# Two written forms for each expert turn of the second layer

## The chip, the core and the metric

The kernel runs on one core of one Trainium2 chip. The metric is the device time of one execution in microseconds. TensorE (PE) multiplies, ScalarE (ACT) and VectorE (DVE) work on rows, GpSimd (POOL) has nothing to do in the stage that is changed, and SyncE (SP) issues the loads of weights. Each engine runs its own list of instructions in order, by its own sequencer, and waits for the others at semaphores. A branch on a value known only at run time is taken by every engine for itself.

## The reference, cut to what matters

A block of two layers; each mixes tokens and then sends every token to two of sixteen experts. The change concerns the experts of the second layer, where only the 256 latent tokens are left.

```python
def moe_ffn(h, w_router, router_bias, w_gate, w_up, w_down):
    ...   # best group of four experts, then the two best experts in it; gates sum to one
    y = jnp.zeros_like(h)
    for e in range(N_EXPERTS):                      # 16
        a = jax.nn.silu(h @ w_gate[e]) * (h @ w_up[e])   # 1024 -> 512
        y = y + gates[..., e:e + 1] * (a @ w_down[e])    # 512 -> 1024
    return y
```

Everything is float32. An expert's weights are 6 MB.

## The kernel before

The second layer's experts are `turns()` (L1808), sixteen turns in the fixed order `TURNS`, one expert a turn. An expert works only on the rows routed to it, in blocks of 64 (`BLK`). How many rows it has is known at run time: `next_count` (L1790) loads the count `cv` into a register on every engine and gives a hint for the coming branch (L1793).

The pieces of a turn: `mm_in` (L1466) multiplies a block of 64 rows with gate and up weights (16 calls, which the trace shows as 32 matmul records); `act` (L1479) makes silu, product and gate on ScalarE and VectorE; `spin` (L1484) transposes the result; `mm_out` (L1491) multiplies with the down weights (16 records in the profile); `where` (L1502) makes the mask of rows, by one matmul into the bank "md", of which there is one, and one VectorE instruction; `parts` (L1509) splits the product in two on VectorE and ScalarE; `add` (L1520) scatters it into the 256 rows by four matmuls and four VectorE additions. `four_fetch` (L1054) gathers a quarter of the first blocks of the next four experts, and `fetch` (L1437) gathers a second block.

A plain turn is pipelined by hand: `mm_in` of expert p with the adds of expert p-2 between (`owed`), `act`, the one-hot of the next expert, `four_fetch`, `where`, `next_count(p + 1)`, `spin`, then `mm_out` of expert p-1 (`previous()`, L1821). The weights come through rings of 1 MB tiles: `main.done(4, 2)` frees the four gate and up tiles after `mm_in`, `main.done(2)` the two down tiles of the expert before, and each frees loads that SyncE issues.

A second block of an expert is `rest` (L1796), behind the branch `cv > BLK` (L1798) at the head of the turn: fetch, `mm_in`, `act`, `where`, `spin`, `mm_out`, `parts`, `add` one after the other, with blocks over 128 behind another branch (L1805, `overflow`). The expert's first block follows, with the same weights. The last turn runs its first block ahead of the branch.

The first layer's turns (`turn_0`, L1607) have two written forms already: one branch (L1672) whose first form treats two or more blocks and whose second form, `branch.Else()`, one. There the hint (`ahead()`, L1665) stands at the end of a turn, next to the branch. `main.repeat()` issues in the second form the loads that `main.done` issued in the first; with `main.again` a ring's tile is used again under its name, so that both forms mean the same tile.

## Time and profile before

| | us |
|---|---|
| median of three runs (1374.8 to 1388.9) | 1385.39 |
| the profiled execution | 1378.21 |
| its span, first to last instruction | 1376.4 |
| TensorE busy in the span | 1186.1 (86%) |
| VectorE busy | 545.2 (40%) |
| mean granted TensorE clock | 0.931 |

The second layer's experts run from 1089 us to 1368 us of the span. In the rows, a line such as L1474 is the helper that issued an instruction, not the caller; PEq or PEldq is TensorE's sequencer. An f32 matmul is listed as PE, its weight load as PEld. The time in brackets on a timeline is the idle time of the engine ahead of the group, and what ended it.

### The profile page before, as it was taken

How to read it: one execution, taken by the hardware profiler on the slowest of the kernel's cores; microseconds unless marked ns; L12 is line 12 of the kernel's file. 1: busy time of each engine (PE TensorE's matmuls, PEld its weight loads, DVE VectorE, ACT ScalarE, POOL GpSimd, SP SyncE). 2: the span in 40 equal slices, each digit the busy share in tenths (PEclk: the TensorE clock that was granted, in tenths of full speed). 3: DMA queues.
4: the chain of work that ended last, by engine and by line, in shares of the span. 5: the costliest groups of instructions: out<-in, count | busy, mean ns of one | idle time of the engine just before them, and what ended most of it. 6: DMA issues, size and time to landing. Idle time of an engine off the chain costs nothing. (4 is left out here: it accounts for less than half of the span.)

```text
span 1376.4 us, 16893 instructions
## 1 busy us (share of the span) xinstructions
PE 1186.1 (86%) x6325; PEld 668.3 (49%) x6325; DVE 545.2 (40%) x1115; ACT 311.2 (23%) x564; POOL 314.0 (23%) x254
## 2 busy tenths in 40 slices
PE   6799999999899878988898995879987698989995
PEld 2466556677678633323333333656775433333331
DVE  5431843834522450110010038585443434434445
ACT  2422213312111311111111125314332111111112
POOL 4332102233022612111111045432335100000000
PEclk9999899999689979999999997989988799989998
DMA  9574333342375489399999835210155298958971
GB/s 356 197 268 180 103 142 108 122 154 92 138 261 214 157 313 341 86 382 386 390 389 393 338 109 220 90 64 16 64 223 229 85 366 335 418 215 338 399 309 47
DMA packets 48579, 310.91 MB, mean 226 GB/s; under 512 B 6017, under 2 KB 6209, under 8 KB 14096
## 3 DMA queue, kind: packets, MB, share of 16 engines
q1 hardware_dynamic: 41936, 292.76, 54.9%
q0 software_dynamic: 6320, 15.27, 4.3%
q8 instruction: 108, 1.77, 0.5%
q10 hardware_dynamic: 144, 0.52, 0.1%
q14 instruction: 71, 0.58, 0.1%
HBM read 297.99 MB, written 12.32 MB: 225 GB/s over the span
## 5 line engine op out<-in xcount | busy, mean ns | idle before, releaser
L576 POOL TENSOR_TENSOR ws<-w,ws 128x1024 fp32r<-128x1024 f32 x50 | 120.5, 2425 | 244.0 <-ACT ws L575 240.5
L1474 PE MATMUL b_pj<-w,HE 128*64 128x512 f32 x416 | 106.2, 646 | 24.1 <-issue 13.8
L235 PE MATMUL b_pj<-hh,ws 128*128 128x512 f32 (+1 forms) x448 | 124.0, 367 | 2.0 <-POOL ws L576 2.0
L1498 PE MATMUL b_sc<-w,rows 128*64 128x512 f32 x448 | 105.2, 610 | 2.7 <-ACT rows L1488 2.7
L666 DVE SCALAR_TENSOR_TENSOR cacc<-gl,pr,cacc 128x512 f32<-128x512 f32 (+1 forms) x120 | 91.2, 760 | 2.4
L235 PEld LDWEIGHTS b_pj<-hh,ws 128*128 128x128 f32 x448 | 79.7, 199 | 20.6 <-issue 8.7
L235 PE MATMUL b_pj<-hl,ws 128*128 128x512 f32 (+1 forms) x224 | 78.9, 352 | 0.0
L1474 PEld LDWEIGHTS b_pj<-w,HE 128*64 128x64 f32 x416 | 34.1, 147 | 84.5 <-issue 82.1
L575 ACT ACTIVATE ws<-w 128x1024 fp32r<-128x1024 f32 x50 | 52.5, 1051 | 77.4 <-PE b_pj L235 50.2
L278 POOL TENSOR_TENSOR rf<-rf,half 128x1 f32<-128x1 f32 x2 | 1.1, 561 | 297.4 <-DVE rf L277 297.4
L1536 DVE TENSOR_TENSOR x<-b_ob,x 128x512 f32<-128x512 f32 x68 | 44.0, 686 | 54.8 <-PE b_ob L1527 54.6
L1381 POOL DMA_INDIRECT sums<-y,rws x19 | 29.8, 1567 | 138.3 <-DVE y L1380 113.5
L1498 PEld LDWEIGHTS b_sc<-w,rows 128*64 128x64 f32 x448 | 31.3, 140 | 60.8 <-issue 56.3
L1474 PE MATMUL b_pj<-w,hf 128*64 128x512 f32 x224 | 56.0, 633 | 5.5 <-PEq L1798 4.9
L1474 PE MATMUL b_pj<-w,x 128*64 128x512 f32 x224 | 55.6, 618 | 5.7 <-PEq L1798 2.8
L235 PE MATMUL b_md<-w,sT 128*32 128x256 f32 x736 | 57.0, 434 | 1.3 <-DVE mT L314 1.3
L1481 DVE SCALAR_TENSOR_TENSOR X<-X,gc,b_pj 64x512 f32<-64x512 f32 x16 | 12.1, 754 | 108.9 <-ACT X L1480 108.9
L1380 DVE COPY y<-b_sc 128x512 f32<-128x512 f32 x15 | 10.4, 691 | 98.4 <-PE b_sc L1498 57.0
L235 PEld LDWEIGHTS b_pj<-hl,ws 128*128 128x128 f32 x224 | 44.5, 199 | 5.8
L1527 PE MATMUL b_ob<-st,ohT 128*128 128x512 f32 x76 | 32.3, 494 | 14.8 <-DVE st L1517 9.3
L1480 ACT ACTIVATE X<-b_pj 64x512 f32<-64x512 f32 x16 | 9.4, 589 | 157.0 <-PE b_pj L1474 150.8
L1480 ACT ACTIVATE cst<-b_pj 64x512 f32<-64x512 f32 x17 | 10.1, 592 | 141.4 <-PE b_pj L1474 141.4
(471 smaller groups left out, 2154.4 us busy)
## 6 DMA issues: line engine op xcount, KB each, us to landing
w<-in_exps_dram SPq DMA_DIRECT2D x168, 1024.0 KB
w<-in_ada_dram SPq DMA_DIRECT2D x48, 1024.0 KB
w<-in_win_dram SPq DMA_DIRECT2D x16, 1024.0 KB
hold<-in_exps_dram SPq DMA_DIRECT2D x12, 1024.0 KB
w<-in_wout_dram SPq DMA_DIRECT2D x8, 1024.0 KB
hf<-in_exps_dram SPq DMA_DIRECT2D x6, 1024.0 KB
cst<-in_exps_dram SPq DMA_DIRECT2D x6, 1024.0 KB
pr<-in_par_dram SPq DMA_DIRECT2D x2, 1461.5 KB
```

The costliest lines, as they stand in the source:

```text
L235: nc.tensor.matmul(out_, lhsT=lhsT, rhs=rhs, **kw)
L575: nc.scalar.activation(wh[:, :n], src, AF.Copy)
L576: nc.gpsimd.tensor_tensor(wl[:, :n], src, wh[:, :n].bitcast(F32), op=OP.subtract)
L666: nc.vector.scalar_tensor_tensor(ac, gl[:, :, j:j + L], R("cvw", i * 31 + j, i * 31 + j + 1), ac, op0=OP.mult, op1=OP.add)
L1380: V.tensor_copy(y, b)
L1381: nc.gpsimd.indirect_dma_start(out=sums[:, :], out_offset=bass.IndirectOffsetOnAxis(ap=row, axis=0), in_=y, in_offset=None, bounds_check=1 ...
L1474: nc.tensor.matmul(b[64 * j:64 * j + 64], lhsT=x, rhs=w[k // 2][:, at:at + 512], start=(k == 0), stop=(k == 7), tile_position=(0, 64 * j))
L1480: nc.scalar.activation(a[64:], b[:64], AF.Silu)
L1481: V.scalar_tensor_tensor(a[64:], a[64:], gate[64:], b[64:], op0=OP.mult, op1=OP.mult)
L1498: nc.tensor.matmul(b[64 * j:64 * j + 64], lhsT=aT[:, f, :], rhs=w[4 + f // 2][:, at:at + 512], start=(f == 0), stop=(f == 3), tile_positio ...
L1527: nc.tensor.matmul(b, lhsT=ohT[:, t * P:(t + 1) * P], rhs=st[h], start=(i == 0), stop=(i == len(blocks) - 1))
L1536: V.tensor_tensor(y[:, cs], b, y[:, cs], op=OP.add)
```

## The change

Each turn becomes one branch with two written forms. When the count is over 64, both blocks run interleaved: `first()` (matmul, adds, act of the first block), `fetch`, the second block's `mm_in` with the same gate and up weights, then mask, transposes, the second matmuls of the expert before and of the second block, adds, and blocks over 128 behind an inner branch. Otherwise (`branch.Else()`) the old plain turn. The last turn has the branch at its head as well. `next_count(p + 1)`, which loads the count and gives the hint, moves from ahead of `spin` to behind the two forms, so it is the last thing in a turn, next to the branch of the next. `main.done(2)` moves behind the forms too. In the form for two blocks the loads that follow the freed gate and up tiles are issued at its end, in the other one by `main.repeat()` where they were. The one-hot tiles of the second block are used again (`into=oh1`) instead of allocated, and the whole of `turns()` is issued in the order in which it is written.

```diff
--- before.py
+++ after.py
@@ -1793,71 +1793,100 @@
                 tc.mark_branch_hint_location(f"rest{p}", cv > BLK, engines=engs)
                 return cv
 
-            def rest(p, e, cv, w, oh1, last):
-
-                with tc.If(cv > BLK, label=f"rest{p}"):
-                    at, st, o = AT[(p + last) % 2], ST[p % 2], OT[(p + last) % 3]
-                    with tc.manual_schedule(engines=PE_):
-                        a1 = act(mm_in(w, fetch(oh1)), gc[:, 1, e:e + 1], AM[(p + 1) % 2])
-                        where(e, o, C("slot", 1, 2), "md")
-                        b = mm_out(w, spin(a1, at))
-                    add((parts(b, st), o))
-                    with tc.If(cv > P):
-                        overflow(e, w, cv, P, AM[(p + 1) % 2], at, st, o, into=oh1)
+            def rest(e, cv, w, oh1, temp):
+
+                with tc.If(cv > P):
+                    overflow(e, w, cv, P, *temp, into=oh1)
 
             def turns():
 
 
+
+                main.again = True
                 w = aT = owed = before = None
                 oh1 = onehot(TURNS[0], C("iota2"), off1, name="on")
-                with tc.manual_schedule(engines=ALL):
-                    cv = next_count(0)
+                cv = next_count(0)
                 for p, e in enumerate(TURNS):
                     last = p == NE - 1
                     now, nxt = four[p // 4 % 2], four[(p // 4 + 1) % 2]
                     pw, pT, w = w, aT, [main.take("exp", l, 6 * e + q) for q in range(6)]
                     x = [q[:, :, p % 4] for q in now[0]]
-
-                    def previous(between=None):
-                        b = mm_out(pw, pT, bank("sc"), between)
-                        main.done(2)
+                    o, a0, aT = OT[p % 3], AM[p % 2], AT[p % 2]
+
+                    a1, st1, o1 = AM[(p + 1) % 2], ST[(p + 1) % 2], OT[(p + 1) % 3]
+
+                    def previous():
+                        b = mm_out(pw, pT, bank("sc"))
                         return parts(b, ST[p % 2]), before
 
-                    if last:
-                        with tc.manual_schedule(engines=ALL):
-                            b0 = mm_in(w, x, between=lambda k: k in (4, 6) and add(owed, only=[k // 2 - 2]))
-                            a0 = act(b0, gc[:, 0, e:e + 1], AM[p % 2])
-                            was = where(e, OT[p % 3], C("slot", 0, 1), "md")
-                            owed = previous()
-                            aT = spin(a0, AT[p % 2])
-                            b = mm_out(w, aT, bank("sc"), lambda f: f > 1 and add(owed, only=[f - 2]))
-
-                            owed = parts(b, ST[(p + 1) % 2]), was
-                        rest(p, e, cv, w, oh1, True)
-                        with tc.manual_schedule(engines=ALL):
-                            add(owed)
-                            main.done(6)
-                        break
-                    rest(p, e, cv, w, oh1, False)
-                    with tc.manual_schedule(engines=ALL):
-                        if p % 4 == 0 and p < NE - 4:
-                            four_onehots(nxt[1], pd, p // 4 + 1)
+                    def first():
                         b0 = mm_in(w, x, between=lambda k: owed and k in (4, 6) and add(owed, only=[k // 2 - 2]))
-                        main.done(4, 2 if p else 0)
-                        a0 = act(b0, gc[:, 0, e:e + 1], AM[p % 2])
-                        oh1 = onehot(TURNS[p + 1], C("iota2"), off1, name="on")
+                        act(b0, gc[:, 0, e:e + 1], a0)
+
+                    def second(h):
+
+                        b1 = mm_in(w, h, tag="md")
+                        act(b1, gc[:, 1, e:e + 1], a1)
+
+                    def end():
+
+                        b = mm_out(w, aT, bank("sc"), lambda f: f > 1 and add(now_owed, only=[f - 2]))
+                        add((parts(b, ST[(p + 1) % 2]), o))
+
+                    if p % 4 == 0 and p < NE - 4:
+                        four_onehots(nxt[1], pd, p // 4 + 1)
+                    with tc.If(cv > BLK, label=f"rest{p}") as branch:
+                        first()
+                        h = fetch(oh1)
+                        second(h)
+                        where(e, o, C("slot", 0, 1), "md")
+                        spin(a0, aT)
                         if p < NE - 4:
                             four_fetch(nxt[0], hx, nxt[1], [p % 4])
-                        was = where(e, OT[p % 3], C("slot", 0, 1), "md")
-                        cv = next_count(p + 1)
-                        aT = spin(a0, AT[p % 2])
+                        t1 = spin(a1, h[:, :4])
                         if p:
                             now_owed = previous()
+                        b = mm_out(w, t1, bank("sc"))
+                        if last:
+                            add(now_owed)
+                        where(e, o1, C("slot", 1, 2), "md")
+                        add((parts(b, st1), o1))
+                        rest(e, cv, w, oh1, (a1, AT[(p + 1) % 2], st1, o1))
+                        if last:
+                            b = mm_out(w, aT, bank("sc"))
+                            add((parts(b, st1), o))
+                            main.done(8)
+                        else:
+                            main.done(4, 2 if p else 0)
+                            onehot(TURNS[p + 1], C("iota2"), off1, into=oh1)
+                    with branch.Else():
+                        first()
+                        if last:
+                            where(e, o, C("slot", 0, 1), "md")
+                            now_owed = previous()
+                            spin(a0, aT)
+                            end()
+                            main.repeat()
+                        else:
+                            main.repeat()
+                            onehot(TURNS[p + 1], C("iota2"), off1, into=oh1)
+                            if p < NE - 4:
+                                four_fetch(nxt[0], hx, nxt[1], [p % 4])
+                            where(e, o, C("slot", 0, 1), "md")
+                            spin(a0, aT)
+                            if p:
+                                now_owed = previous()
+                    if last:
+                        break
+                    if p:
+                        main.done(2)
+                    cv = next_count(p + 1)
                     owed = now_owed if p else None
-                    before = was
+                    before = o
 
             if l:
-                turns()
+                with tc.manual_schedule(engines=ALL):
+                    turns()
             if dump is not None:
                 for t in range(T):
                     dump(f"x{l}_{t}", xres[t])
```

## Rows read from the trace of the kernel before

**Rows 1.** Busy time by stretch: PE, PEld, DVE, ACT, POOL busy (instructions), granted clock, DMA share, GB/s

```profile
1089.28:1210.63 121.35, 112.37 (x496) 43.36 (x497) 46.70 (x80) 17.75 (x32) 0.00 (x0) 0.96 0.90 361
1210.63:1252.82 42.19, 36.15 (x157) 15.01 (x155) 13.71 (x23) 5.62 (x11) 0.00 (x0) 0.88 0.56 217
1252.82:1341.97 89.15, 83.43 (x373) 29.94 (x375) 40.31 (x68) 13.99 (x25) 0.00 (x0) 1.00 0.88 354
```

**Rows 2.** Timeline of TensorE, 1263 to 1282: start us, duration, instruction [hole before]

```profile
1263.41 3.65 PE L1498 MATMUL b_sc<-w,rows 128*64 128x512 f32 x16
1267.37 3.65 PE L1474 MATMUL b_pj<-w,hf 128*64 128x512 f32 x16 [0.31 <-PEq L1798]
...
1281.92 3.65 PE L1474 MATMUL b_pj<-w,hf 128*64 128x512 f32 x16 [0.31 <-PEq L1798]
```

**Rows 3.** TensorE's sequencer by line, 1258 to 1268: ns min/median/max, first and last start

```profile
L1792 PEldq TENSOR_LOAD <-cnt x1: 307/307/307, 1260.3 to 1260.3; - x1
...
L2065 PEldq BRANCH_PREFETCH_HINT  x1: 35/35/35, 1260.8 to 1260.8; - x1
...
L1798 PEldq COMPARE_BRANCH  x1: 2387/2387/2387, 1263.4 to 1263.4; - x1
```

**Rows 4.** The turns' branches: whole stage, then 1206 to 1208, then the first

```profile
L1798 PEldq COMPARE_BRANCH  x16: 82/3452/6124, 1085.3 to 1360.1; - x16
...
L1798 PEldq COMPARE_BRANCH  x1: 82/82/82, 1207.1 to 1207.1; - x1
...
L1798 PEldq COMPARE_BRANCH  x1: 3741/3741/3741, 1085.3 to 1085.3; - x1
```

**Rows 5.** First layer's branches: 600 to 790, and one border (735 to 744)

```profile
L1672 PEldq COMPARE_BRANCH  x11: 89/6076/6708, 600.8 to 772.3; - x11
...
L2065 PEldq BRANCH_PREFETCH_HINT  x1: 35/35/35, 737.3 to 737.3; - x1
...
L1672 PEldq COMPARE_BRANCH  x1: 6196/6196/6196, 737.8 to 737.8; - x1
```

**Rows 6.** Timeline of TensorE in the first layer, two restarts of eight

```profile
672.41 7.93 PE L1474 MATMUL b_pj<-w,HE 128*64 128x512 f32 x28 [2.33 <-DMA w<-in_exps_dram]
...
729.19 6.23 PE L1474 MATMUL b_pj<-w,HE 128*64 128x512 f32 x28 [2.81 <-issue]
```

**Rows 7.** Waits, 1085 to 1377 (us in total, times, longest); then timeline of TensorE

```profile
PE b_pj L1474 <- PEq L1798: 12.2, 9, 4.2
...
PE b_pj L1474 <- ACT st L1516: 3.2, 2, 1.6
...
PE b_pj L1474 <- DMA w<-in_exps_dram: 1.0, 2, 0.7
...
1099.54 0.46 PE L1487 MATMUL b_tp<-cst 64*128 64x64 f32 x4
...
1149.85 5.35 PE L1474 MATMUL b_pj<-w,x 128*64 128x512 f32 x16 [2.81 <-PEq L1798]
```

**Rows 8.** Timeline of TensorE, 1215 to 1241: the one second block, then its expert's first

```profile
1215.29 3.65 PE L1474 MATMUL b_pj<-w,hO 128*64 128x512 f32 x16
...
1222.30 0.38 PE L1505 MATMUL b_md<-pdT,pick 16*128 16x256 f32 x1
1224.05 0.46 PE L1487 MATMUL b_tp<-cst 64*128 64x64 f32 x4 [1.37 <-DVE cst L1481]
1224.98 5.35 PE L1498 MATMUL b_ob<-w,rows 128*64 128x512 f32 x16 [0.47 <-ACT rows L1488]
1232.60 0.47 PE L1527 MATMUL b_ob<-st,ohT 128*128 128x512 f32 x1 [2.27 <-DVE st L1517]
...
1236.21 5.41 PE L1474 MATMUL b_pj<-w,hf 128*64 128x512 f32 x16 [0.54 <-PEq L1805]
```

**Rows 9.** Timeline of TensorE in the last two turns

```profile
1336.23 1.93 PE L1474 MATMUL b_pj<-w,x 128*64 128x512 f32 x6
...
1364.77 0.71 PE L1527 MATMUL b_ob<-st,ohT 128*128 128x512 f32 x2 [3.10 <-DVEq L1798]
```

## The prediction

> **What bounds the kernel now.** I read three views of the last stage in this order. First the busy time by stretch [rows 1]: the stage starts at 1089.28 us, and TensorE is busy 112.4 of its first 121.4 us and 83.4 of 89.2 us after the one long turn, VectorE 39% and 45%. The reader is to see that TensorE's own list of instructions sets the pace and that only its holes can be won. Second TensorE's timeline across one turn border [rows 2]: the last work of a turn is the second matmul of the expert before (16 records, 3.65 us), and the next turn's first matmul stands 0.31 us behind its end; a plain turn is 14.24 us of work, 14.55 us in all (1267.37 to 1281.92). Third what TensorE's sequencer does there [rows 3]: it loads the count at 1260.3, gives the branch hint at 1260.8 and comes to the branch at 1263.4, when the 3.65 us of matmuls are queued but have only begun. The branch lasts 2.39 us and so ends 1.3 us before those matmuls do. It costs nothing because of that cover.

> The sum below is made against the profiled execution, 1378.2 us; the median of the three runs is 7.2 us above it, and I put the same change on that median.

> **What the branch costs.** All sixteen branches of the stage [rows 4]: from 0.08 to 6.12 us, median 3.45. The 0.08 us one is the only one not taken (1207.1), so exactly one expert of sixteen has more than 64 rows, the ninth turn's; fifteen turns jump. For a jump, hint to end is 2.6 + 3.45 = 6.1 us in the middle and 5.0 us in the shortest steady case [rows 3]. The hint therefore takes about 2.6 us off the branch.

> The change moves count load and hint behind the second matmul's instructions, directly ahead of the branch. The first layer is written that way already: a turn with two forms, the hint 0.5 us ahead of the branch [rows 5]. There the jumps last 6.1 us in the middle, up to 6.7, and the branch also starts as the last matmuls begin. TensorE then restarts at most 2.81 us after its last matmul in the eight borders of this kind between 624 and 762 us, on average 2.45 [rows 6]. I take 2.5 us for each new border: 6.1 us of branch and 0.1 to start, less 3.65 of cover.

> [...]

> **The clock behind such a hole.** In the first layer six of those eight restarts are slow: 28 matmuls take 7.93 us after a hole of 2.33 us, but 6.23 us after the one of 2.81 [rows 6]. The six lose 1.25 to 1.9 us, mean 1.66, so 1.25 us for each border on average. In the second layer the hole of 2.81 us is followed by 16 matmuls in 5.35 us instead of 3.65 [rows 7]. [...]

> **The sum, first form.** Holes ahead of a turn's first matmul now, first turn apart: 12.2 - 4.2 = 8.0 us put down to the branch, 3.2 and 1.0 us of the same kind put down to other engines [rows 7], together 12.2; 0.6 of them belongs to the tenth turn, counted below, which leaves 11.6. After the change twelve borders (into turns 3 to 8 and 11 to 16) have 2.5 us each, 30.0. The border into the second turn has no second matmul as cover: its last transposes end at 1100.0 [rows 7], the branch starts about there, and the hole is 6.2 us. Together 36.2, so **+24.6 us**. The clock: 12 x 1.25 = 15.0, less 2.3 that turns 3 and 5 lose now (0.57 and 1.70, the latter in rows 7), **+12.7 us**. The first turn has its hint directly at the branch before and after: 0.

> Free, and what hides it: the count load itself (0.31 us) lies under the second matmuls, else 0.4 us a turn; the one-hot of the next expert keeps its place on VectorE. SyncE re-issues the same four loads at the same place. The last two loads of a turn go behind the join of the forms, so one of them can start up to 1.8 us later; TensorE waits only 1.0 us in all for weights now [rows 7], and turns 3.7 us longer leave more room. Once the cover is gone a late load costs what it is late, at most 1.8 us a turn, which would need the loads to set the pace.

> **The sum, second form.** It runs once. From the second block's fetch to the tenth turn's start is 42.2 us now [rows 1]. In that lie waits: 1.37 and 0.47 us around the transposes, 2.27 ahead of the adds, 0.54 at the inner branch, and two slow stretches of 1.7 us (5.35 and 5.41 us for 16) [rows 8]. Interleaved, step by step: the first block's matmul and adds 8.65 us (as in a plain turn), fetch 4.66 (1210.63 to 1215.29), second block's matmul 7.0, then a new wait: the mask matmul of the first block wants the one "md" bank that the second block's product sits in, so it waits for ScalarE and VectorE, 1.65 us as they took after 1222.30. Behind it on TensorE stand the transposes, everything else. Then mask 0.4, transposes 0.4, next group's fetch 1.1, transposes 0.4, two second matmuls 3.6 each, mask 0.4, and the last block's scatter: 3.2 us wait (2.27 plus VectorE's mask ahead of it, 0.9) and 3.1 of adds. That is 37.6. Behind it the next branch has no cover at all: inner branch 0.5, jump 0.2, count and hint 0.5, branch 6.1, a hole of 7.3, and 1.7 us of clock. Together 46.6: **+4.4 us**. The interleaving wins about 4 us of waits and the border gives back 8.

> **The end.** The sixteenth turn has a branch ahead of it which it had not, counted above; six matmuls that ran early in a VectorE wait (1336.23, [rows 9]) lose that, +1.2. The branch between the last product and the adds is gone: the 3.10 us wait there becomes 2.27, -0.8. **+0.4 us**.

> Sum: 24.6 + 12.7 + 4.4 + 0.4 = **+42 us**: 1420 against this execution, **1427** on the median.

> **The rivals.** *The short fetch.* Loads keep the DMA engines less busy in longer turns, and a jump takes 5.0 us as in rows 3; the hole is 1.5 us, and holes of 1.33 to 1.60 us are followed by full speed now. Then 12 x 1.5 + 5.1 - 11.6 = +11.5, clock -2.3, second form +3.3, end +0.4: +13, 1398. For it: that one row; against: the median of 6.1.

> *Not slower: the jump fits under the cover.* Below 3.9 us a branch hides under the second matmuls, and this decides all. The stage's first jump, with no weights moving, took 3.74 [rows 4]. Holes 13 x 0.3 - 11.6 = -7.7, clock -3.8 (with the second turn's), second form -2.9, end +0.4: -14, 1371. Against it: every jump of the first layer from 624 to 762 us is above 5.8. [...]

> *The forms must be evened out by waiting.* Behind each skipped block TensorE now waits for its own last matmul before it goes on. Were that placed at the first form's end, ahead of the count load, no branch would have cover: holes of 6.8 us, 4.3 more for thirteen borders and the clock each time, about +100, 1487. Against it: the first layer's branch begins while matmuls still run.

> **How the numbers follow.** Forecast 0.65, short fetch 0.17, hidden jump 0.08, evened out 0.10. The forecast's own ends: holes of 2.81 with every restart slow, 12 x 2.81 + 6.5 - 11.6 + 12 x 1.66 - 2.3 + 5.4 = +52, 1437; below, the short fetch's +13. The range runs from 1392 (short fetch on a quicker baseline, whose runs spread from 1374.8 to 1388.9) to 1446 (a few longer jumps like 6.7 us). One per cent, 14 us, is about what the runs can tell from no change. The hidden jump lies on that bound, 0.05 faster and 0.03 same; of the short fetch 0.10 is same, the rest slower: 0.05, 0.13, 0.82.

> **What would show it.** In the profile after: TensorE's branch at the turn's head lasting about 6 us fourteen times and 0.1 us once; holes of 2 to 3 us ahead of the first matmul; a granted clock below 1 over 1253 to 1342; the long turn some 38 us up to its last add and a hole near 7 behind it. The prediction is wrong if the jumps are under 4 us, if the branch is not reached before the last matmuls, or if the long turn gains over 10 us.

## The result and the profile after

The changed kernel takes 1422.11 us in the median (1414.75 to 1423.2, 4 runs) against 1383.52 for the kernel before beside it: a ratio of 1.028 [1.023, 1.033]. Forecast were 1427 us, 42 us more than before. The profiled execution took 1423.2 us, its span is 1421.4 us instead of 1376.4, its mean granted clock 0.916 instead of 0.931.

First the stretches of the changed stage, columns as in [rows 1]: up to the ninth turn's work, the long turn, the tenth to the fifteenth turn, and then the whole stage from its first to its last matmul.

```profile
1089.98:1231.73 141.75, 117.36 (x497) 44.60 (x499) 49.18 (x84) 16.62 (x29) 0.00 (x0) 0.90 0.81 314
1231.73:1279.65 47.92, 33.18 (x156) 14.51 (x153) 15.85 (x27) 6.87 (x13) 0.00 (x0) 0.84 0.36 137
1279.65:1383.59 103.94, 86.00 (x367) 30.25 (x367) 40.73 (x68) 13.39 (x24) 0.00 (x0) 0.96 0.82 322
1089.98:1412.38 322.40, 260.53 (x1097) 97.06 (x1097) 118.88 (x199) 41.18 (x73) 0.00 (x0) 0.91 0.68 264
```

The whole stage of the kernel before, same view:

```profile
1089.28:1367.41 278.13, 251.62 (x1097) 94.64 (x1097) 115.12 (x192) 42.91 (x77) 0.00 (x0) 0.96 0.77 306
```

The same 1097 records of matmuls take 44.3 us longer: TensorE idles 322.40 - 260.53 = 61.9 us instead of 26.5 (35.4 more), and is busy 8.9 us longer with the same work, at a granted clock of 0.91 instead of 0.96. No stretch is at 1.00 any more, as the third of [rows 1] was.

One border, TensorE's timeline; it answers to [rows 2]:

```profile
1292.82 3.65 PE L1498 MATMUL b_sc<-w,rows 128*64 128x512 f32 x16
1299.60 3.65 PE L1474 MATMUL b_pj<-w,hf 128*64 128x512 f32 x16 [3.12 <-issue]
```

TensorE's sequencer at this border, which answers to [rows 3] (the turn's branch is now L1838):

```profile
L1792 PEldq TENSOR_LOAD <-cnt x1: 303/303/303, 1292.8 to 1292.8; - x1
...
L2094 PEldq BRANCH_PREFETCH_HINT  x1: 35/35/35, 1293.4 to 1293.4; - x1
...
L1838 PEldq COMPARE_BRANCH  x1: 5958/5958/5958, 1293.5 to 1293.5; - x1
```

The count is loaded as the last matmuls begin, the hint and the branch follow 0.6 and 0.7 us later, and the jump outlasts the 3.65 us of matmuls: the hole of 0.31 us has become 3.12. In the kernel before the branch started as those matmuls began (1263.4 and 1263.41, [rows 3] and [rows 2]). All branches of the stage, and the one into the tenth turn, which answer to [rows 4], and the inner branch ahead of the code for rows over 128:

```profile
L1838 PEldq COMPARE_BRANCH  x17: 85/5729/6422, 1086.2 to 1378.6; - x17
...
L1838 PEldq COMPARE_BRANCH  x1: 6422/6422/6422, 1273.1 to 1273.1; - x1
...
L1798 PEldq COMPARE_BRANCH  x1: 3312/3312/3312, 1268.6 to 1268.6; - x1
```

The median is 5.73 us instead of 3.45; the 0.085 us one is the only one not taken, ahead of the long turn. Holes and restarts, TensorE's timeline, which answers to [rows 7]; then the view of waits, where these holes are put down to "issue":

```profile
1108.24 9.99 PE L1474 MATMUL b_pj<-w,hf 128*64 128x512 f32 x32 [6.13 <-issue]
...
1126.88 5.35 PE L1474 MATMUL b_pj<-w,hf 128*64 128x512 f32 x16 [3.01 <-issue]
...
1145.41 1.08 PE L1474 MATMUL b_pj<-w,hf 128*64 128x512 f32 x4 [2.54 <-issue]
...
PE b_pj L1474 <- issue: 50.5, 15, 10.2
```

"Issue" is idle time in which TensorE waited for no semaphore: its sequencer sat in the branch. The 50.5 us hold the thirteen holes of the plain turns (36.2), the 10.23 us behind the long turn and the 4.03 us ahead of the first. The long turn, TensorE's timeline, which answers to [rows 8]:

```profile
1231.73 1.46 PE L1474 MATMUL b_pj<-w,hf 128*64 128x512 f32 x6
...
1252.87 0.38 PE L1505 MATMUL b_md<-pdT,pick 16*128 16x256 f32 x1 [1.48 <-DVE cst L1481]
...
1255.80 4.46 PE L1498 MATMUL b_sc<-w,rows 128*64 128x512 f32 x16
1260.10 3.60 PE L1498 MATMUL b_sc<-w,hO 128*64 128x512 f32 x16
...
1266.57 0.50 PE L1527 MATMUL b_ob<-st,ohT 128*128 128x512 f32 x1 [2.56 <-DVE st L1517]
...
1279.65 1.12 PE L1474 MATMUL b_pj<-w,hf 128*64 128x512 f32 x2 [10.23 <-issue]
```

From its first matmul to its last add it takes 37.7 us (1231.73 to 1269.42). The wait for the one "md" bank is there (1.48 us), the waits around the second block's transposes are gone, the one ahead of the adds stays (2.56 us), and the hole behind the turn is 10.23 us.

One wait is new outside the borders. In the first turn the transposes now wait 1.47 us for VectorE, which waits for ScalarE: its table load ran at 1086.2 in the kernel before, during the stage's first jump, and now stands behind the wait for the first product. TensorE's wait after, then ScalarE's table load before and after:

```profile
1101.65 0.46 PE L1487 MATMUL b_tp<-cst 64*128 64x64 f32 x4 [1.47 <-DVE cst L1481]
...
1086.18 1.28 ACT L1480 ACT_TABLE_LOAD   x1 [0.67 <-ACTq L1798]
...
1098.84 1.28 ACT L1480 ACT_TABLE_LOAD   x1 [12.47 <-PE b_pj L1474]
```

### The profile page after: what moved, and what is told of

It is laid out like the page before. It is cut to its first block, busy times and chain, and to the rows that moved or that the text cites. A ratio compares the mean times of both kernels' runs of the same rounds, so it can differ in the third digit from the quotient of the medians.

```text
span 1421.4 us, 16908 instructions
## 1 busy us (share of the span) xinstructions
PE 1196.7 (84%) x6325; PEld 672.4 (47%) x6325; DVE 549.7 (39%) x1120; ACT 307.9 (22%) x559; POOL 313.3 (22%) x254
## 5 line engine op out<-in xcount | busy, mean ns | idle before, releaser
L1474 PE MATMUL b_pj<-w,hf 128*64 128x512 f32 x224 | 59.1, 668 | 26.2 <-issue 26.2
L1474 PE MATMUL b_pj<-w,x 128*64 128x512 f32 x224 | 59.1, 661 | 15.9 <-issue 15.9
L1498 PEld LDWEIGHTS b_sc<-w,rows 128*64 128x64 f32 x448 | 31.3, 140 | 61.0 <-issue 55.8
L1481 DVE SCALAR_TENSOR_TENSOR X<-X,gc,b_pj 64x512 f32<-64x512 f32 x16 | 12.1, 753 | 111.0 <-ACT X L1480 111.0
L1474 PEld LDWEIGHTS b_pj<-w,hf 128*64 128x64 f32 x224 | 18.0, 151 | 60.7 <-issue 60.3
L1527 PE MATMUL b_ob<-st,ohT 128*128 128x512 f32 x76 | 32.1, 491 | 14.1 <-DVE st L1517 12.1
```

What stands on the lines that cost most here:

```text
L1474: nc.tensor.matmul(b[64 * j:64 * j + 64], lhsT=x, rhs=w[k // 2][:, at:at + 512], start=(k == 0), stop=(k == 7), tile_position=(0, 64 * j))
L1481: V.scalar_tensor_tensor(a[64:], a[64:], gate[64:], b[64:], op0=OP.mult, op1=OP.mult)
L1498: nc.tensor.matmul(b[64 * j:64 * j + 64], lhsT=aT[:, f, :], rhs=w[4 + f // 2][:, at:at + 512], start=(f == 0), stop=(f == 3), tile_positio ...
L1527: nc.tensor.matmul(b, lhsT=ohT[:, t * P:(t + 1) * P], rhs=st[h], start=(i == 0), stop=(i == len(blocks) - 1))
```

## The experiments

All times are medians beside the kernel before on the same chip. The first theory is the prediction's: the hint has come too near to the branch, the jump outgrows its cover, and the holes take the clock down with them. Its rival: the two written forms cost it themselves, wherever the hint stands.

### The late hint alone, in the old form

```diff
-                        cv = next_count(p + 1)
                         aT = spin(a0, AT[p % 2])
                         if p:
                             now_owed = previous()
+                        cv = next_count(p + 1)
```

> The kernel before, one written form, with only the count load and the hint moved behind the second matmuls, directly ahead of the next branch. If the place of the hint makes the holes: jumps of about 6 us, holes of 1 to 3.4 us at eleven borders and about 6 at the second turn, +22 us of holes and +11 of clock, some 3 to 4 more behind the second block: about 1418. If the two written forms make them (longer jump, join): unchanged, 1380 to 1386.

Measured: 1412.17 us, ratio 1.025 [1.019, 1.031], 6 us under the expected 1418. The turns' branches and the stage's windows row:

```profile
L1798 PEldq COMPARE_BRANCH  x15: 85/5842/6444, 1095.5 to 1393.6; - x15
```

```profile
1084.60:1400.86 316.26, 260.48 (x1097) 96.23 (x1097) 114.96 (x192) 42.90 (x77) 0.00 (x0) 0.93 0.70 269
```

One line moved down makes +30 us without a second form: the median jump is 5.84 us instead of 3.45, and TensorE idles 55.8 us instead of 26.5 and is busy 8.9 us longer, as in the changed kernel. That the late place of count load and hint makes such holes is shown, at 30 of the 39 us; the two move together here.

### The early hint in the two forms

The count is loaded two turns ahead, so that the hint can stand in front of the transposes again, 3.5 us ahead of the branch in most turns.

```diff
                             where(e, o, C("slot", 0, 1), "md")
+                            hint(p + 1, ncv)
                             spin(a0, aT)
...
-                    cv = next_count(p + 1)
+                    cv = ncv
+                    if p + 2 < NE:
+                        ncv = next_count(p + 2)
```

> The changed kernel with counts loaded a turn earlier and the hint back ahead of the transposes in the form for one block (ahead of the second block's second matmul in the other). If the place of the hint makes the holes: jumps of 1.4 to 6.1 us again, holes 12 us in sum instead of 36, and 1378 to 1386. If the two forms make them: 1418 to 1424 as the changed kernel.

Measured: 1409.52 us, ratio 1.021 [1.015, 1.028], in neither of the two ranges: the time did not come back. Two branches and all of them, from the sequencer's rows:

```profile
L1841 PEldq COMPARE_BRANCH  x1: 752/752/752, 1123.2 to 1123.2; - x1
...
L1841 PEldq COMPARE_BRANCH  x1: 6007/6007/6007, 1153.7 to 1153.7; - x1
...
L1841 PEldq COMPARE_BRANCH  x16: 88/4455/6213, 1105.0 to 1369.5; - x16
```

Their hints were given at 1118.3 and 1150.2, 4.9 and 3.5 us ahead. One took effect, the other did nothing: its jump of 6.01 us is as long as those with the hint at the branch (5.73 us in the middle in the changed kernel). Nine of the thirteen jumps of plain turns (the second to the eighth and the eleventh to the sixteenth; so counted below too) are longer than 3.9 us. So my theory was incomplete: a hint is taken up only sometimes. The kernel before had shown one such case, which I read over: into its fifth turn the jump lasted 6.12 us, the maximum in [rows 4], with the hint 2.7 us ahead, as long as a jump with the hint at the branch.

```profile
L2065 PEldq BRANCH_PREFETCH_HINT  x1: 35/35/35, 1140.7 to 1140.7; - x1
...
L1798 PEldq COMPARE_BRANCH  x1: 6124/6124/6124, 1143.4 to 1143.4; - x1
```

### The hint at the head of each form

As above, but the hint is the first thing in each form, 12 to 14 us ahead.

> The changed kernel with the hint of the next branch as the first thing in each form, some 12 us ahead of it. If code that is asked for early waits ready: every hole 0.3 us, no slow restart, 1365 to 1374. If an early hint is lost behind the code that is fetched in sequence meanwhile: jumps of about 6 us, 1418 to 1424.

Measured: 1399.42 us, ratio 1.013 [1.007, 1.018], again between the two ranges.

```profile
L1841 PEldq COMPARE_BRANCH  x17: 88/466/6181, 1092.4 to 1366.6; - x17
```

The jumps fall into two kinds: eight of thirteen last 0.35 to 0.47 us, five (into turns 2, 5, 8, 11 and 15) 5.9 to 6.2. More lead makes a hint that takes effect worth the whole jump; four turns fewer are lost than at 3.5 us, but five still are.

### The hint a whole turn ahead, in the old form

The kernel before, with the count loaded two turns ahead and the hint at the head of a turn's block; in the built program it lies directly ahead of the branch before, some 14.5 us early in most turns.

```diff
                     with tc.manual_schedule(engines=ALL):
+                        hint(p + 1, ncv)
                         if p % 4 == 0 and p < NE - 4:
...
-                        cv = next_count(p + 1)
+                        cv = ncv
+                        if p + 2 < NE:
+                            ncv = next_count(p + 2)
```

> The kernel before, one form, with counts loaded two turns ahead and the hint at the head of the turn, some 12 us ahead of its branch instead of 2.6. If a hint is always taken up once it is early enough: holes of 0.3 us, no slow restart, about 1369. If it is lost in some turns by where the code lies, as in the run with the hint at the head of two forms (5 of 13 lost there): jumps of 0.4 us beside jumps of 6, 1385 to 1400.

Measured: 1367.61 us (1359.61 to 1371.89), ratio 0.988 [0.981, 0.995]: faster than both kernels. The branches and the stage's windows row:

```profile
L1800 PEldq COMPARE_BRANCH  x15: 80/374/5258, 1097.4 to 1346.3; - x15
```

```profile
1087.22:1354.30 267.08, 247.49 (x1097) 92.81 (x1097) 115.97 (x194) 42.91 (x77) 0.00 (x0) 0.97 0.79 318
```

Jumps of 0.37 us in the middle, one long one (5.26 us, so one hint is lost here too); TensorE idles 19.6 us instead of 26.5. The kernel before was losing part of its jumps as well, which its holes of 12.2 us in [rows 7] had shown.

### The hint a whole turn ahead, in the two forms, and the same without the code for more rows

```diff
+                    hint(p + 1, ncv)
                     with tc.If(cv > BLK, label=f"rest{p}") as branch:
```

> The changed kernel's two forms, each count loaded two turns ahead and the hint for a turn's branch given directly ahead of the branch of the turn before, some 15 us early, as it came to lie in the one-form kernel that ran at 1367.6 us. If a hint needs only time, every jump lasts 0.3 to 0.6 us, the holes are 0.3 us, and the time is that kernel's less the 4 us that the long turn gains: 1360 to 1372 us. If the two written forms lose hints whatever their lead, as at 3.5 us (1409.5) and at 12 us (1399.4), four or five of thirteen jumps still last about 6 us and the time is 1390 to 1405 us.

> As the two-form kernel with the hint a whole turn ahead, with the code for an expert's rows over 128 left out (no expert here has so many), which shortens the skipped form by about half. If a hint needs only time: all jumps under 0.6 us, 1358 to 1370 us, like its longer sibling. If the length of the skipped form decides which hints are lost: fewer long jumps than its longer sibling, at most two of thirteen, 1365 to 1378 us (1373.8 with the hint 3.5 us ahead).

Measured: 1392.6 us, ratio 1.003 [0.999, 1.006], for the first; 1370.2 us, ratio 0.990 [0.986, 0.995], for the second, whose profiled execution (1382.55 us) lies 12 us above its median, so only its jumps are read. The branches of the first, and its jump into the fifth turn:

```profile
L1842 PEldq COMPARE_BRANCH  x17: 83/455/6152, 1085.1 to 1349.4; - x17
...
L1842 PEldq COMPARE_BRANCH  x1: 6152/6152/6152, 1147.1 to 1147.1; - x1
```

The branches of the second:

```profile
L1841 PEldq COMPARE_BRANCH  x17: 92/375/6241, 1091.2 to 1341.4; - x17
```

The first came out as its second case has it. With a turn's lead the two forms still lose four hints of thirteen, in turns 2, 5, 8 and 15, which are turns that lost theirs at 12 us too: lead alone does not do it. The second missed: in the profiled execution the shorter one loses four as well (turns 4, 8, 12 and 15), not two at most. That execution is one of four at 1381 to 1385 us; the other six take 1365 to 1371, and how many hints are lost in those no trace shows. It has no hole of 5.92 us into the second turn (0.68 us there) and no inner branch behind the long turn, which is followed by a hole of 0.69 us instead of 6.42.

### Code that never runs

The two-form kernel with the hint a turn ahead, plus 51 matmuls behind the code for rows over 128, which no expert here reaches.

```diff
                     overflow(e, w, cv, P, *temp, into=oh1)
+                    junk = bank("md")
+                    for _ in range(51):
+                        nc.tensor.matmul(junk[:BLK], lhsT=ident[:, :BLK], rhs=hx[0][:, 0, :512].bitcast(F32), start=True, stop=True)
```

> The two-form kernel with the hint a whole turn ahead (1392.6 us; jumps of 5.6 to 6.2 us in turns 2, 5, 8 and 15, under 0.9 in the other plain ones), with 51 matmuls that never run written behind the code for rows over 128, so that each turn's code is some 205 instructions longer (about 821 to 1026, by the kernel's listing) and nothing that runs is added. If something in a turn itself, its loads or its work, loses the hint, the same turns 2, 5, 8 and 15 have the long jump and the time stays at 1388 to 1397 us. If where the code lies decides, other turns are lost, and since the new length is close to four of the 16,384-byte pieces in which code is fetched, the plain turns 3 to 12 all go alike: all jumps under 0.9 us (1368 to 1378 us) or nearly all at 6 us (1410 to 1425 us).

Measured: 1378.72 us, ratio 0.998 [0.993, 1.002]; without the dead code it was 1.003 [0.999, 1.006]. The same 1097 matmul records run in the stage, in 276.6 us instead of 291.7. All branches, and the jump into the fifth turn, which took 6.15 us above:

```profile
L1845 PEldq COMPARE_BRANCH  x17: 80/443/5965, 1088.5 to 1338.5; - x17
...
L1845 PEldq COMPARE_BRANCH  x1: 457/457/457, 1149.5 to 1149.5; - x1
```

The lost turns moved: 2, 5, 8 and 15 are now all under 0.5 us, and 3 and 11 lost (5.86 and 5.96). The turns' work and loads are the same, so they do not by themselves decide which hints take effect; what was changed is the code's layout (its place, or the length of the jump, which grew with it). The expectation's four pieces to a turn are an estimate: between 45 and 440 us of the kernel before, the code queue took 19 packets while TensorE went through 4623 matmuls and weight loads, 243 for each, and by that 1026 instructions are 4.2 packets. That turns 3 to 12 all go alike did not hold: 3 and 11 are long, 5 to 8 short, and 4 and 12 are at 2.1 to 2.2 us, which still hides under the 3.65 us of cover. The two ratios' intervals overlap, so a gain in the whole time is not shown.

Each kernel was traced in one execution, so chance is a rival that no run rules out. Against it stands that in kernels with nearly the same code each list of lost turns lies within the one before: with the long form 2, 4, 5, 8 and 11 to 15 at 3.5 us, then 2, 5, 8, 11 and 15 at 12 us, then 2, 5, 8 and 15 at a turn's lead. The rule by which a hint is lost stays open.

### The skipped code made short

The changed kernel without the code for an expert's rows over 128 (no expert here has so many), once with its late hint, once with the hint 3.5 us ahead.

```diff
             def rest(e, cv, w, oh1, temp):
-                with tc.If(cv > P):
-                    overflow(e, w, cv, P, *temp, into=oh1)
+                pass
```

> The changed kernel, hint late, with the code for rows over 128 left out (no expert of these inputs has them). If only the distance from hint to branch counts: holes of 1 to 3.4 us as in the changed kernel, 1412 to 1424 (the tenth turn's hole 3 us shorter). If it counts how far the jump goes: in some turns the target is fetched already and the jump takes 0.4 us, 1385 to 1405.

> The two forms with the early hint, and the code for rows over 128 of an expert (which no expert of these inputs has) left out: the first form is shorter by more than half, what runs is the same. If the early hint was lost because of where the longer first form puts the target: fewer long jumps, 1370 to 1390. If joins or waits of the two forms themselves cost it: 1404 to 1412 as with the longer form.

Measured: 1381.95 us, ratio 1.001 [0.997, 1.005], with the late hint; 1373.77 us, ratio 0.997 [0.994, 1.000], with the early one. The branches of the first, then of the second:

```profile
L1837 PEldq COMPARE_BRANCH  x16: 82/538/6023, 1096.3 to 1336.8; - x16
...
L1840 PEldq COMPARE_BRANCH  x16: 89/450/6018, 1087.5 to 1330.5; - x16
```

The late hint, which cost 2.8% with the long form, costs nothing that the runs can tell with the short one, 3 us below the expected range. Some 9.5 of the 40 us between the two are the border behind the long turn, which has no inner branch here (a hole of 0.68 us instead of 10.23). So the hint's place makes the loss only together with the length of what is jumped across, or the place of the code that goes with it.

With the hint 0.09 us ahead of the branch, six of thirteen jumps last 0.36 to 0.62 us and no piece of code is fetched during them; the others take 3.35 to 6.02. A packet of code takes about 1 us (0.93 to 1.09 in the changed kernel's plain jumps into turns 2 to 15), so a hint so late can't have fetched anything, and in those turns the target was there already. That it lay in a piece that had been fetched in sequence is what I argue, not what a row says; that code also comes without a branch is shown, 19 packets of it between 45 and 440 us of the kernel before, where no engine takes one. In the second run eight of thirteen are short; its five long ones (turns 4, 5, 8, 13 and 16) are among the seven of the first (4, 5, 8, 12, 13, 15 and 16), and so are the four of the short form with a turn's lead. The changed stage took 37 packets on the code queue, 0.61 MB, each of 16,384 bytes.

### More work in front of the jump

The changed kernel with 3, or 2, matmuls of no use ahead of `previous()`, to lengthen the cover. They write into a bank that the turn uses itself ("md", or "tp"), so they wait for it as well as adding work.

```diff
                             if p:
+                                junk = bank("md")
+                                for _ in range(3):
+                                    nc.tensor.matmul(junk, lhsT=ident, rhs=hx[0][:, 0, :512].bitcast(F32), start=True, stop=True)
                                 now_owed = previous()
```

> The changed kernel with three matmuls without use (128x512, into a bank that nobody reads) ahead of the second matmuls in the form for one block: 2.5 us more work that is queued when the branch is reached. If the holes are a jump longer than its cover and the slow restarts come from the holes: holes of 0.3 to 0.9 us, the restarts at full speed, and about 10 to 12 us less, 1410. If the clock falls whatever TensorE does there, or the hole stays on top: 1422 to 1455.

> The changed kernel with two matmuls without use (2.8 us by the 4.27 that six records took in the run with three) into the transposes' bank, whose wait is there anyway. If the slow restarts come from the holes: the same work and hole in sum, every restart at full speed, 9 to 12 us less than the changed kernel: about 1411. If not: 1422 or more.

Measured: 1470.38 us, ratio 1.067 [1.061, 1.074], with three; 1443.51 us, ratio 1.045 [1.037, 1.052], with two. A border of the first, TensorE's timeline:

```profile
1173.67 4.54 PE L1880 MATMUL b_md<-hxh,cst 128*128 128x512 f32 x6 [1.42 <-DVE ohT L1506]
1178.13 3.65 PE L1498 MATMUL b_sc<-w,rows 128*64 128x512 f32 x16
1182.32 3.23 PE L1474 MATMUL b_pj<-w,x 128*64 128x512 f32 x14 [0.53 <-issue]
```

And of the second:

```profile
1155.80 1.98 PE L1880 MATMUL b_tp<-hxh,cst 128*128 128x512 f32 x4 [0.53 <-ACT rows L1488]
1157.71 1.94 PE L1498 MATMUL b_sc<-hf,rows 128*64 128x512 f32 x8
...
1163.35 2.76 PE L1474 MATMUL b_pj<-w,x 128*64 128x512 f32 x10 [1.98 <-issue]
```

The filler bought no cover, and both times lie far above the hoped-for 1410. The branch starts 0.66 us after the 3.65 us of matmuls begin (1178.79), in the other run 0.63 us (1158.34), and in the changed kernel 0.61 to 0.80 (0.61 at 1156.66, 0.65 at 1293.47): the sequencer reaches it at that distance, however much work stands ahead.

In the run with three, ten of thirteen jumps last only 3.4 to 3.8 us and leave holes of 0.3 to 0.8. Ten holes under 1 us and one of 1.90 are followed by full speed, those of 2.10 and 5.70 by 5.35 and 5.20 us for 16 records. In the second run six of thirteen jumps still last 4.8 to 6.5 us.

The DMA queues during single jumps say why they differ: the changed kernel's into turn 13 (6.08 us, 1326.34 to 1332.42) and into turn 15 (4.05 us, 1362.93 to 1366.98), and the one into turn 11 in the run with three (3.36 us, 1318.71 to 1322.07). q1 carries the weights, q8 the code; packets, MB and share of the 16 engines:

```profile
q1 hardware_dynamic: 353, 2.55, 99.8%
q8 instruction: 1, 0.02, 1.1%
...
q1 hardware_dynamic: 148, 1.08, 77.3%
q8 instruction: 1, 0.02, 1.5%
...
q1 hardware_dynamic: 75, 0.48, 44.7%
q8 instruction: 1, 0.02, 1.8%
```

Each of the three holds one packet of code, of 16,384 bytes. In the changed kernel and the other runs with a late hint, plain turns 3 to 16, such a packet starts 0.9 to 1.2 us after the branch where weights take up to 0.62 of the DMA engines during the jump, 1.6 to 2.1 us after it at 0.75 to 0.84, and 2.3 to 4.0 us after it at 0.88 or more; the packet takes about 1 us, and the jump ends 1.4 to 1.6 us behind it. That makes jumps of 3.3 to 3.8, 3.9 to 4.5 and 4.8 to 6.5 us. Two jumps of 4.85 us fetched two packets and fall outside this, and the short jumps fetched none. That the code's packet queues behind those of the weights is the reading that fits; no row names what it waits for.

### The count load alone moved early

The changed kernel with the count loaded two turns ahead and the hint left at the branch.

> The changed kernel with only the count loaded two turns ahead; the hint stays directly ahead of the branch. If the jump alone sets the hole, the load of 0.31 us lies under the last matmuls and nothing is won: jumps of about 6 us, holes of 2.5 to 3.4 us, 1418 to 1424 us. If the count load adds to the path (branch reached 0.4 us earlier in every turn), holes shrink by 0.4 us in thirteen turns and the time is 1413 to 1418 us.

Measured: 1424.09 us, ratio 1.030 [1.023, 1.038]: nothing won, the median jump is 5.79 us. The second case was not tested by this edit: a load, now of the count after next, still stands between the last matmuls and the hint, and the branch still starts 0.62 us after those matmuls begin (1115.68 against 1115.06).

## Why the prediction was right, and where it fell short

The time (1427 against 1422) and the mechanism held: a jump that outlasts its cover leaves a hole, and the clock falls behind some of the holes. The total is closer than its terms, whose errors offset each other in part. By the prediction's own terms, in the profiled execution:

| term | forecast | measured |
|---|---|---|
| holes into thirteen plain turns | 36.2 - 11.6 = +24.6 | 36.2 - 12.0 = +24.3 |
| clock behind them | +12.7 | +8.5 |
| first turn | 0 | +1.4 |
| long turn and the border behind it | +4.4 | +8.2 |
| end | +0.4 | +1.7 |
| sum | +42 | +44.1 |

The stage grew by 44.3 us and the span by 45.0; 0.7 of that is the stage's start, 1089.98 instead of 1089.28. The medians lie 38.6 us apart. The 11.6 left out one hole of before, which the view of waits puts down to a load:

```profile
PE b_pj L1474 <- DMA hf<-in_exps_dram: 0.3, 1, 0.3
```

*Holes.* The seven into turns 2 to 8 sum to 22.25 us (6.13, 3.01, 2.54, 3.42, 1.08, 3.21, 2.86), the six into turns 11 to 16 to 13.99 (3.12, 1.19, 3.22, 3.12, 1.19, 2.15). That 2.5 us for each of twelve came out is luck: two errors cancel. The twelve jumps last 5.35 us in the mean, not 6.1 (eight 5.4 to 6.3 us, three 3.95 to 4.06 and one 4.85); of all fifteen taken branches ten last over 5.4 us, where fourteen of about 6 were to show it. And the time ahead of the branch, which "Free, and what hides it" put at nothing, is in every hole: the branch starts 0.66 us in the mean after the last matmuls begin, where load and hint now stand, so 0.66 + 5.35 + 0.16 to start - 3.65 is 2.5. In the first layer, from which the 2.5 was taken, the branch starts 0.2 us ahead of its cover (737.8 in [rows 5]):

```profile
738.04 3.60 PE L1498 MATMUL b_sc<-w,rows 128*64 128x512 f32 x16
```

*Clock.* Five of twelve restarts were slow, by 1.70, 2.77, 1.70, 1.67 and 1.70 us, 9.5 together (5.35 us for 16 records instead of 3.65, and so on; the granted clock was 0.56 to 0.68 over them, and 1.00 over the fast ones), where I had 1.25 us for each of twelve. The restart into the second turn took 9.99 us for its 32 records against 8.78 before, 1.2 more, and 2.3 of before are gone. The holes of 2.54 and of 3.12 us were followed by full speed, the one of 2.15 was not, so a hole's length does not settle it by itself.

*First turn.* From its first matmul to its last transpose it takes 12.1 us instead of 10.7: the table load, which the prediction did not look at.

*Long turn.* Up to its last add 37.7 us against 37.6 forecast, waits included (the steps as the prediction lists them add up to 38.2). The mis-sized term is the border behind it: the hole is 10.23 us instead of 7.3, because the inner branch took 3.31 us, where I had 0.5, from a kernel in which it took 0.35. It jumps across the code for rows over 128, and its target has to be fetched like any other (one packet of code starts 0.99 us into it): 2.51 us of it lie behind the last add, then 1.14 until the turn's branch starts, 6.42 of that branch, and 0.16 to start. The slow restart (6.18 us for 16) took 2.5 instead of 1.7, and it does not come from that hole: in the run with a turn's lead and without the code for more rows it is as slow behind a hole of 0.69 us (granted clock 0.59 over those 16 records, 0.58 in the changed kernel).

```profile
1250.13 6.09 PE L1474 MATMUL b_pj<-w,hf 128*64 128x512 f32 x16 [0.69 <-issue]
```

The interleaving itself wins what was said: without the jump, in that run, the long turn with its border is 38.4 us (1211.74 to 1250.13) against 42.2 before.

*End.* From the last turn's first matmul to the last one 28.8 us against 25.4, of which 1.7 is the slow restart counted above. The adds' wait fell to 2.17 us as forecast; a second slow stretch (3.35 us for 8 records at 1400.46) was not in the sum.

*The rivals.* The short fetch fell as a forecast, since only four of thirteen jumps were under 5.4 us; but its reason was sound, and three of those four are jumps during which weights took 0.78 to 0.83 of the DMA engines. The hidden jump fell in this code, but holds wherever the target is there: 0.34 to 0.48 us, in a few cases up to 0.81. The branch not taken lasted 0.085 us, the shortest taken one 0.34. Evening out by waiting did not happen: the branches start while matmuls run.

*The step that fell short* is "What the branch costs": it put the jump down to the hint's place alone, and took 2.6 us for the hint's gain from the median, where single jumps of before with 2.6 to 2.7 us of lead last from 2.4 to 6.1 us. The late hint alone costs 30 us and the two forms with an early hint 27, but both together 39, as if a jump were lost only once. Undoing the hint's move did not bring the time back, which the prediction's wording would have had; leaving out skipped code that never runs did, with the hint as late as ever (ratio 1.001 instead of 1.028).

## What to carry to other kernels

A branch that is taken across much code costs TensorE a fetch, here 4.8 to 6.5 us while weights took 0.88 or more of the DMA engines; read in the sequencer's rows when the hint, the branch and the last matmuls ahead of it begin, because only the difference is free and whatever stands between cover and branch adds to the hole (here 0.66 us). Load the value a turn earlier and give the hint a whole turn ahead: in the one-form kernel that was worth 1.2% over the kernel before. Then look at each jump by itself, since a few lost hints hide in a median, and keep code that hardly runs (here for rows over 128) out of the stretch that is jumped across: without it the changed kernel ran at 1382 us instead of 1422. The runs left that code out, and such a kernel would be wrong for an expert with over 128 rows; putting it elsewhere was not tried.
